# First modulation columns shared with TensorE, modulation weights in a buffer of their own on GpSimd's queue, bias rows in 16 copies

## Chip, cores and metric

One core of a Trainium2 chip runs the program. The metric is device time in microseconds, as the median of the executions shown. Lines named L… are lines of the kernel before, as its profile numbers them.

## What is computed

Two transformer blocks of two layers each run on 256 tokens of width 1024, all in float32. Of the reference, this part matters:

```python
c_act = silu(c)
for l in range(2):
    mod = c_act @ w_ada[l] + b_ada[l]                      # [1, 6144]
    sh1, sc1, gt1, sh2, sc2, gt2 = split(mod, 6)
    h = modulate(rms_norm(x, norm_mix[l]), sh1, sc1)
    p = h @ w_in[l]                                        # attention, RWKV, gated MLP, gates
    ...
    x = x + gt1 * (merged @ w_out[l])
    h = modulate(rms_norm(x, norm_ffn[l]), sh2, sc2)
    x = x + gt2 * conv_gated_ffn(h, ...)
```

The second block has no modulation. Its window attention adds `rel_bias[t5_buckets(k - q)]` to the scores, and its last step adds `(p @ w_pe_proj) * sigmoid(...)`.

## The kernel before, in words

**Products.** Activations lie with features on the partitions. A weight tile of 128x1024 comes from HBM over SP's queue into a slot `raw` (`wload`, L122 to L142). ScalarE rounds it to `hi` (L137), VectorE forms the rest `lo` (L138), and TensorE makes three products for each pair of tiles (L164 to L166), each 128x128 weights by 256 columns. The slots `raw` and `hi`/`lo` come from a ring over the open pools (`ring`): 3 `raw` and 4 splits in the mixing stages, 6 and 7 in the two feed-forward stages of the first block.

**Modulation.** A column group f (128 of the 6144 outputs) takes one 128x1024 tile of `w_ada`, which VectorE multiplies with `cact` (silu of c on all partitions) and sums along the row (L338, in the start L369). The first 16 groups of layer 0 are made at the start in `LayerA`, in 8 tiles of 1 MB on SP's queue. The other 32 of layer 0 and the 48 of layer 1 are background tasks (`ada_task`, L330 to L339): `tick` lets 0.67 of one run behind each `wload`, and `need` runs what is left up to a key before the columns are used (L389, L402). Each task takes a `raw` slot of the ring, issues its load on SP's queue (L337) and its product on VectorE right behind it.

**Start.** c comes in one row, goes through silu on ScalarE and is spread by TensorE (L1337 to L1341). The squares of x are summed on VectorE (L222), then over the partitions on TensorE (L228). `modulated` (L409 to L418) multiplies x with 1/rms (L415), applies scale and shift (L416) and splits (L201, L202). Weights 12, 6 and 10 are loaded ahead, and `fmulti` multiplies them with the contraction outermost, so that it can begin with the first of the eight tiles of h.

**Feed-forward stage of layer 0** (`ffn_a`, 372 to 617 us). `project` (L1260 to L1281) fills TensorE while the norm is under way: it splits `pT` and writes four products to DRAM over ScalarE's queue, in four buffers of the tag `pj`, three of which hold `pT`, `hi` and `lo`. Before pair 8 of 22 `hook` calls `bias_rows` (L1001 to L1015): one product gives the bias of 8 heads by distance on 8 partitions, and one DMA on ScalarE's queue writes it to DRAM with 128 copies of each row, 2 MB in all. `bias_table` (L1018 to L1024) later reads it back, shifted by one for each query, in two DMAs of 1 MB on SP's queue.

**Order of work.** Python order gives priorities, and the tile framework places each engine's instructions at build time, by its own idea of when each is ready. Each engine then runs its list in order: a VectorE instruction that waits for a DMA holds all that is behind it.

## Time and profile before

| what | value |
|---|---|
| median of 3 executions | 2324.88 us (2322.84 to 2325.23) |
| the profiled execution: span, which is the time that the profile gives for it | 2323.2 us |
| TensorE busy (matmul) | 2240.6 us, 96% |
| VectorE, ScalarE busy | 72%, 55% |
| GpSimd busy | 0.2 us |
| moved by DMA | 416.69 MB, mean 179 GB/s |

The page gives the busy time of each engine and the chain of work that ended last. A table by stretches then gives the busy time, the number of matmuls and the granted clock in a piece of the span. The order in time on one engine shows how long it stood idle before each instruction and what ended that.

### The profile page before, as it was taken

What the parts mean: (1) busy time and instruction counts of PE and PEld (TensorE: products, weight loads), DVE (VectorE), ACT (ScalarE), POOL (GpSimd) and SP (SyncE); (2) the same over time, 40 slices, a digit from 0 to 9 for tenths busy, and PEclk for the clock granted to TensorE, in tenths of its full rate; (3) what the DMA queues carried; (4) which work ended last, traced back from release to release, by engine and by line L of the source; (5) the groups of instructions that cost most, each with busy time, mean ns of one, the idle gap of its engine ahead of it and who ended that gap; (6) DMA issues with size and microseconds to landing.
All of it is one profiled execution on the core that took longest, in us unless ns stands there. A gap on an engine that the chain in (4) does not pass through costs nothing.

```text
span 2323.2 us, 46766 instructions
## 1 busy us (share of the span) xinstructions
PE 2240.6 (96%) x19122; PEld 2142.4 (92%) x19122; DVE 1677.5 (72%) x3026; ACT 1276.9 (55%) x2144; POOL 0.2 (0%) x4
## 2 busy tenths in 40 slices
PE   4999998978999999999999999999999999999999
PEld 4888898978888889999999999899999999999999
DVE  7777767757677776877576659976667655997665
ACT  4574545544457464565454457654455446666444
POOL 0000000000000000000000000000000000000000
PEclk9999999989999999999999999999999999999999
DMA  7634457777663445875576563466565556346653
GB/s 294 190 118 128 142 177 242 250 199 231 191 199 116 137 129 167 266 228 159 169 237 182 161 208 109 131 211 186 156 210 183 174 168 200 109 138 216 183 158 124
DMA packets 129117, 416.69 MB, mean 179 GB/s; under 512 B 14564, under 2 KB 20324, under 8 KB 128134
## 3 DMA queue, kind: packets, MB, share of 16 engines
q1 hardware_dynamic: 126718, 409.50, 55.8%
q10 hardware_dynamic: 2184, 4.19, 0.9%
q8 instruction: 150, 2.46, 0.4%
q14 instruction: 65, 0.53, 0.1%
HBM read 408.40 MB, written 5.24 MB: 178 GB/s over the span
## 4 chain that ended last, share of the span: by engine, by line
PE 80%; DMA 8%; DVE 7%; ACT 4%; issue 1%; SPq 0%; ACTq 0%; DVEq 0%
PE ps L164 23%; PE ps L165 22%; PE ps L166 22%; DMA raw<-in_ffn_up 3%; DVE lo L138 2%; DMA raw<-in_w_ada 2%; ACT hi L137 1%; DMA raw<-in_w_in 1%; PE rec L582 1%; PE rec L590 1%; DVE raw L369 1%; PE rec L1178 1%; DVE raw L338 1%; PE rec L636 1%; PE ps L191 1%
## 5 line engine op out<-in xcount | busy, mean ns | idle before, releaser
L164 PE MATMUL ps<-h,hi 128*128 128x256 f32 x5080 | 1438.4, 284 | 31.9 <-ACT h L201 29.6
L166 PE MATMUL ps<-h,lo 128*128 128x256 f32 x5080 | 1433.4, 283 | 14.7 <-DVE lo L138 14.7
L165 PE MATMUL ps<-l,hi 128*128 128x256 f32 x5080 | 1435.7, 283 | 4.9 <-DVE l L202 4.7
L137 ACT CAST hi<-raw 128x1024 fp32r<-128x1024 f32 (+1 forms) x724 | 704.7, 977 | 648.4 <-PE ps L165 377.8
L138 DVE TENSOR_TENSOR lo<-raw,hi 128x1024 fp32r<-128x1024 f32 (+1 forms) x724 | 818.9, 1133 | 301.6 <-ACT hi L137 299.0
L164 PEld LDWEIGHTS ps<-h,hi 128*128 128x128 f32 x5080 | 961.0, 190 | 47.2 <-ACT h L201 31.9
L166 PEld LDWEIGHTS ps<-h,lo 128*128 128x128 f32 x5080 | 962.3, 190 | 23.8 <-DVE lo L138 15.7
L165 PEld LDWEIGHTS ps<-l,hi 128*128 128x128 f32 x5080 | 961.8, 189 | 13.9 <-DVE l L202 6.8
L201 ACT CAST h<-t 128x256 fp32r<-128x256 f32 x172 | 68.6, 403 | 122.8 <-DVE t L996 96.1
L338 DVE SCALAR_TENSOR_TENSOR raw<-raw,cact 128x1024 f32<-128x1024 f32 x80 | 97.2, 1215 | 35.4 <-DMA raw<-in_w_ada 35.4
L202 DVE TENSOR_TENSOR l<-t,h 128x256 fp32r<-128x256 f32 x172 | 72.3, 423 | 60.5 <-ACT h L201 59.9
L993 DVE TENSOR_TENSOR t<-ps,r 128x512 f32<-128x512 f32 x88 | 60.8, 690 | 41.7 <-PE ps L166 41.3
L1183 DVE SCALAR_TENSOR_TENSOR cy<-cp,cwh,cy 128x256 f32<-128x256 f32 x192 | 85.0, 476 | 3.2 <-ACT cy L1181 2.9
L215 ACT ACTIVATE t<-x 128x256 f32<-128x256 f32 x96 | 38.5, 407 | 15.4 <-DVE x L964 8.5
L222 DVE TENSOR_TENSOR t<-t,t 128x256 f32<-128x256 f32 x87 | 36.4, 418 | 5.5 <-ACT t L215 4.3
L191 PE MATMUL ps<-hi,l 128*128 128x256 f32 x128 | 37.7, 294 | 0.0
L190 PE MATMUL ps<-hi,h 128*128 128x256 f32 x128 | 37.7, 294 | 0.0
L996 DVE TENSOR_TENSOR t<-t,t 128x256 f32<-128x256 f32 x88 | 36.8, 418 | 1.0 <-ACT t L995 1.0
L995 ACT ACTIVATE t<-t 128x256 f32<-128x256 f32 x88 | 36.2, 411 | 0.9
L192 PE MATMUL ps<-lo,h 128*128 128x256 f32 x128 | 36.7, 287 | 0.0
L960 ACT ACTIVATE t<-t 128x256 f32<-128x256 f32 x44 | 18.1, 415 | 29.0 <-DVE t L959 29.0
L416 ACT ACTIVATE t<-t,sh,am 128x256 f32<-128x256 f32 x32 | 18.1, 595 | 26.0 <-DVE am L395 22.5
(311 smaller groups left out, 1884.3 us busy)
## 6 DMA issues: line engine op xcount, KB each, us to landing
raw<-in_w_in SPq DMA_DIRECT2D x176, 512.0 KB, 4.2
raw<-in_ffn_in SPq DMA_DIRECT2D x176, 512.0 KB, 4.2
raw<-in_ffn_up SPq DMA_DIRECT2D x88, 512.0 KB, 5.4
raw<-in_w_ada SPq DMA_DIRECT2D x84, 512.0 KB, 4.8
raw<-in_ffn_out SPq DMA_DIRECT2D x64, 384.0 KB, 3.1
raw<-in_ffn_out SPq DMA_DIRECT2D x64, 320.0 KB, 3.2
raw<-in_w_branch SPq DMA_DIRECT2D x24, 512.0 KB, 4.1
raw<-in_ffn_down SPq DMA_DIRECT2D x32, 384.0 KB, 3.2
```

The source lines that it names most:

```text
L137: nc.scalar.copy(hi[:, :m], raw[:, :m])
L138: nc.vector.tensor_tensor(lo[:, :m], raw[:, :m], hi[:, :m], SUB)
L164: mm(ps, w[0], x[0], start=first, stop=False)
L165: mm(ps, w[0], x[1], start=False, stop=False)
L166: mm(ps, w[1], x[0], start=False, stop=last)
L191: mm(ps[:, :256], x[k][1][:, sl], h, start=False, stop=False)
L201: nc.scalar.copy(h, src)
L202: nc.vector.tensor_tensor(l, src, h, SUB)
L215: nc.scalar.square(sq, x[k])
L338: nc.vector.scalar_tensor_tensor(raw, raw, 1.0, cact, MUL, MUL, accum_out=mods[f // 8][:, f % 8:f % 8 + 1])
L993: nc.vector.tensor_tensor(v3(gu, 2), v3(ps, 2), rb, MUL)
L1183: stt(y, cp[:, jj:jj + S], cwh[:, jj * 4 + i:jj * 4 + i + 1], y, MUL, ADD)
```

## The change

Five of the 16 column groups of the start (0, 1, 2, 3 and 5) are made by TensorE, eight matmuls of one column each, from tiles that the host lays out the other way; ScalarE copies them out. The 16 tiles come one by one in the order 8, 0, 9, 1, ... with weights 12, 6 and 10 between them. c is read straight to all partitions. Half of x and `vec` come over ScalarE's queue. The sum of squares of the first norm is left to TensorE, 16 matmuls of one column. A background task loads into one buffer `adar` over GpSimd's queue, and its product is put into program order only when the next task runs, or `need` does. `bias_rows` makes 16 copies of the 8 rows in one product and writes 256 KB once; `bias_table` reads 16 pieces of 128 KB over GpSimd's queue. `project` has six buffers (`onehot` and `ohb` share them). For room, the pool `wxa` has 2 `raw` slots in place of 3, the RWKV buffers R, X, Y have 1 and ST 2, and `rkb` is made for each pair. Comments and docstrings are gone, without effect.

```diff
+ADA_BUFS = 1
+ADA_PE = (0, 1, 2, 3, 5)
     def need(self, key):
         while self.bg and self.bg[0][0] <= key:
             self.bg.pop(0)[1]()
+        self.ada_flush()
+    def ada_flush(self):
+        if self.ada_pend:
+            self.ada_pend()
+            self.ada_pend = None
+    def rms_pe(self, x):
+        nc = self.nc
+        ps = self.aux()
+        sqs = []
+        for k in range(8):
+            sq = self.tmp(S)
+            nc.scalar.square(sq, x[k])
+            sqs.append(sq)
+        self.load_ident()
+        for t in range(2):
+            for k, a in enumerate(sqs):
+                nc.tensor.matmul(ps[:, t:t + 1], a[:, t * 128:t * 128 + 128], self.ones[:, 0:1], start=k == 0, stop=k == 7)
+        return self.spread(self.inv_rms(ps[:, :2]), False)
-def ada_task(G, l, f, mods, cact):
+def ada_task(G, l, f, mods, cact, pool):
     def run():
         nc = G.nc
-        p, b = G.ring("raw")
-        raw = p.tile([128, D], F32, tag="raw", bufs=b, name=G.nm("raw"))
-        nc.sync.dma_start(raw, ...)
-        nc.vector.scalar_tensor_tensor(raw, raw, 1.0, cact, ...)
+        G.ada_flush()
+        raw = pool.tile([128, D], F32, tag="adar", bufs=ADA_BUFS, name=G.nm("ada"))
+        nc.gpsimd.dma_start(raw, ...)
+        def product():
+            nc.vector.scalar_tensor_tensor(raw, raw, 1.0, cact, ...)
+        G.ada_pend = product
 class LayerA:
-            for n, j in enumerate((0, 4, 1, 5, 2, 6, 3, 7)):
...
+            for k in range(8):
+                for f in (8 + k, k):
+                    raw = first.tile([128, D], F32, tag="ada", bufs=16, name=G.nm("raw"))
+                    out = self.mods[f // 8][:, f % 8:f % 8 + 1]
+                    if f in ADA_PE:
+                        nc.sync.dma_start(raw, G.ins["w_ada_pe"][ADA_PE.index(f)])
+                        ps = G.rec()
+                        for i in range(8):
+                            nc.tensor.matmul(ps[:, 0:1], raw[:, i * 128:i * 128 + 128], ccol[:, i:i + 1], start=i == 0, stop=i == 7)
+                        nc.scalar.copy(out, ps[:, 0:1])
+                    else:
+                        nc.sync.dma_start(raw, ...)
+                        nc.vector.scalar_tensor_tensor(raw, raw, 1.0, cact, ..., accum_out=out)
+                late(k)
-BUFS = dict(..., R=2, X=2, Y=2, W=2, ST=3, y=2)
+BUFS = dict(..., R=1, X=1, Y=1, W=2, ST=2, y=2)
 def bias_rows(G, pool):
-    sk = G.dr.tile([8, 128, 512], F32, name="skew")
-    nc.tensor.matmul(ps[0:8, :], rel, oh, start=True, stop=True)
-    nc.scalar.dma_start(sk, t.unsqueeze(1).to_broadcast([8, 128, 512]))
+    sk = G.dr.tile([128, 512], F32, name="skew")
+    nc.vector.tensor_copy(v3(rel16, 16), rel.unsqueeze(1).to_broadcast([33, 16, 8]))
+    nc.tensor.matmul(ps, rel16, oh, start=True, stop=True)
+    t = pool.tile([128, 512], F32, tag="pj", name="ohb", bufs=6)
+    nc.scalar.dma_start(sk, t)
 def bias_table(G, pool, sk):
-        G.nc.sync.dma_start(bias[:, :, q, :], src)
+        for a in range(0, 128, 16):
+            src = bass.AP(tensor=sk.tensor, offset=sk.offset + 127 - a + (128 if q == 0 else 0), ap=[[8 * 512 - 1, 16], [512, 8], [1, 256]])
+            G.nc.gpsimd.dma_start(bias[a:a + 16, :, q, :], src)
 def project(G, mp, parts, tag="pj"):
-        return mp.tile([128, 512], dt, tag=tag, name=G.nm("pj"), bufs=4)
+        return mp.tile([128, 512], dt, tag=tag, name=G.nm("pj"), bufs=6 if tag == "pj" else 4)
 def build(...):
-                nc.sync.dma_start(t, ins["x"][:, k, :])
+                (nc.scalar if k % 2 else nc.sync).dma_start(t, ins["x"][:, k, :])
...
+                    nc.sync.dma_start(cact, ins["c"].to_broadcast([128, D]))
+                    nc.scalar.dma_start(ccol, ins["cc"])
                     load_x()
+                    nc.scalar.activation(ccol, ccol, AF.Silu)
+                    nc.scalar.activation(cact, cact, AF.Silu)
+                    def late(k):
+                        if k in (1, 3, 6):
+                            load_w({1: 12, 3: 6, 6: 10}[k])
+                    G.first_rms = G.rms_pe(x)
+                    L = [LayerA(G, 0, lp, cact, sp, late, ccol)]
-                        G.weights(wx, 3, 3)
+                        G.weights(wx, 2, 3)
```

## Rows read from the trace of the kernel before

**Rows 1.** The page: span, engines, chain by engine.

```profile
span 2323.2 us, 46766 instructions
PE 2240.6 (96%) x19122; PEld 2142.4 (92%) x19122; DVE 1677.5 (72%) x3026; ACT 1276.9 (55%) x2144; POOL 0.2 (0%) x4
...
PE 80%; DMA 8%; DVE 7%; ACT 4%; issue 1%; SPq 0%; ACTq 0%; DVEq 0%
```

**Rows 2.** Stretches: from:to, us, busy PE, PEld, DVE, ACT, POOL, clock, DMA share, GB/s.

```profile
372.00:617.00 245.00, 217.98 (x1749) 214.89 (x1748) 170.99 (x289) 118.50 (x187) 0.00 (x0) 0.93 0.74 231
960.00:1178.00 218.00, 214.55 (x1793) 213.39 (x1792) 154.33 (x246) 125.80 (x204) 0.00 (x0) 0.99 0.65 205
```

**Rows 3.** The same view, pieces of the start and of the feed-forward stage.

```profile
0.00:20.00 20.00, 6.87 (x16) 3.87 (x16) 8.45 (x17) 12.05 (x18) 0.20 (x4) 1.00 0.82 291
20.00:40.00 20.00, 8.89 (x54) 8.39 (x55) 19.46 (x51) 6.00 (x12) 0.00 (x0) 1.00 1.02 413
...
500.00:520.00 20.00, 20.00 (x171) 20.00 (x170) 16.98 (x27) 11.71 (x17) 0.00 (x0) 1.00 0.92 314
...
480.00:500.00 20.00, 8.32 (x55) 8.11 (x55) 4.99 (x8) 4.21 (x6) 0.00 (x0) 0.66 0.59 148
548.00:560.00 12.00, 4.85 (x26) 3.86 (x26) 9.08 (x18) 5.57 (x11) 0.00 (x0) 0.76 0.65 191
...
560.00:580.00 20.00, 20.00 (x155) 20.00 (x154) 14.22 (x23) 8.12 (x13) 0.00 (x0) 0.89 0.81 252
```

**Rows 4.** Groups of 0 to 56 us; last product; last of the first matmuls.

```profile
L369 DVE SCALAR_TENSOR_TENSOR raw<-raw,cact 128x1024 f32<-128x1024 f32 x16 | 19.0, 1216 | 0.0
...
L228 PE MATMUL aux<-ones,t 128*128 128x1 f32 x8 | 1.9, 355 | 1.8 <-ACT cact L1341 1.8
...
45.24 1.21 DVE L369 SCALAR_TENSOR_TENSOR raw<-raw,cact 128x1024 f32<-128x1024 f32 x1
52.10 0.28 PE L165 MATMUL ps<-l,hi 128*128 128x256 f32 x1
```

**Rows 5.** Order in time behind the first products: SP's queue.

```profile
58.29 0.34 SPq L337 DMA_DIRECT2D raw<-in_w_ada  x1
60.01 1.46 SPq L133 DMA_DIRECT2D raw<-in_w_in  x2
```

**Rows 6.** Order in time around the norm of the feed-forward stage, VectorE and ScalarE.

```profile
391.75 1.23 DVE L338 SCALAR_TENSOR_TENSOR raw<-raw,cact 128x1024 f32<-128x1024 f32 x1 [1.73 <-DMA raw<-in_w_ada]
...
397.40 0.59 ACT L1280 COPY pj<-ps 128x512 f32<-128x512 f32 x1 [5.10 <-DMA proj<-pj]
```

**Rows 7.** DMA issues of 452 to 485 us: size, median us to landing.

```profile
raw<-in_ffn_up SPq DMA_DIRECT2D x6, 512.0 KB, 18.3
skew<-ohb ACTq DMA_DIRECT2D x1, 2048.0 KB
```

**Rows 8.** Order in time, waits of VectorE and TensorE at 541 to 558 us.

```profile
543.56 1.23 DVE L338 SCALAR_TENSOR_TENSOR raw<-raw,cact 128x1024 f32<-128x1024 f32 x1 [1.93 <-DMA raw<-in_w_ada]
...
553.84 0.39 PE L164 MATMUL ps<-h,hi 128*128 128x256 f32 x1 [3.72 <-ACT h L201]
```

**Rows 9.** The background products: waits, landing, and L338 in a stage (two instructions each).

```profile
  DMA raw<-in_w_ada: 35.4, 21
...
raw<-in_w_ada SPq DMA_DIRECT2D x84, 512.0 KB, 4.8
...
372.00:617.00 245.00, 34.42 (x58) 0.93 0.74 231
```

**Rows 10.** The stretch between the second mixing stage and its feed-forward stage.

```profile
940.00:980.00 40.00, 36.70 (x295) 35.94 (x293) 33.98 (x55) 20.94 (x33) 0.00 (x0) 0.96 0.82 268
```

**Rows 11.** The bias read back, and a weight that ScalarE waits for.

```profile
bias<-skew SPq DMA_DIRECT2D x2, 1024.0 KB, 7.1
...
1182.57 1.04 ACT L137 CAST hi<-raw 128x1024 fp32r<-128x1024 f32 x1 [2.21 <-DMA raw<-in_ffn_in]
```

**Rows 12.** Who waited for whom in the RWKV levels: us, times, longest.

```profile
PE rec L582 <- DVE R L575: 0.7, 2, 0.6
```

More of the change, by code (lines that the diff above doesn't have):

```diff
@@ L327, in v3, with __init__ @@
     return t.rearrange("p (a b) -> p a b", a=a)
[L332 removed]
+def ada_task(G, l, f, mods, cact, pool):
     def run():
         nc = G.nc
[L335 to L338 removed]
+        G.ada_flush()
+        raw = pool.tile([128, D], F32, tag="adar", bufs=ADA_BUFS, name=G.nm("ada"))
+        nc.gpsimd.dma_start(raw, G.ins["w_ada"][l, f // 2, :, (f % 2) * D:(f % 2) * D + D])
+        def product():
+            nc.vector.scalar_tensor_tensor(raw, raw, 1.0, cact, MUL, MUL, accum_out=mods[f // 8][:, f % 8:f % 8 + 1])
+        G.ada_pend = product
     return run
 class LayerA:
[L345 removed]
+    def __init__(self, G, l, pool, cact, first=None, late=None, ccol=None):
         nc = G.nc
@@ L349, in __init__ @@
         self.vec = p.tile([128, NVA], F32, tag="vec", name=G.nm("vec"))
-        nc.sync.dma_start(self.vec, G.ins["va"][l])
+        (nc.sync if first is None else nc.scalar).dma_start(self.vec, G.ins["va"][l])
         self.mods = [p.tile([128, 8], F32, tag=f"mod{i}", name=G.nm("mod")) for i in range(6)]
@@ L356, in __init__ @@
         else:
-            for n, j in enumerate((0, 4, 1, 5, 2, 6, 3, 7)):
-                if n == 6:
-                    late()
-                raw = first.tile([128, 2, D], F32, tag="ada", bufs=8, name=G.nm("raw"))
-                src = v3(G.ins["w_ada"][l, j], 2)
-                if n < 6:
-                    nc.sync.dma_start(raw, src)
-                for h in range(2):
-                    if n >= 6:
-                        nc.sync.dma_start(raw[:, h, :], src[:, h, :])
-                    f = 2 * j + h
-                    nc.vector.scalar_tensor_tensor(raw[:, h, :], raw[:, h, :], 1.0, cact, MUL, MUL, accum_out=self.mods[f // 8][:, f % 8:f % 8 + 1])
-        G.bg += [((l, f), ada_task(G, l, f, self.mods, cact)) for f in range(0 if first is None else 16, 48)]
+            for k in range(8):
[9 more added lines that the diff above has]
+                    else:
+                        nc.sync.dma_start(raw, G.ins["w_ada"][l, f // 2, :, (f % 2) * D:(f % 2) * D + D])
+                        nc.vector.scalar_tensor_tensor(raw, raw, 1.0, cact, MUL, MUL, accum_out=out)
+                late(k)
+        G.bg += [((l, f), ada_task(G, l, f, self.mods, cact, p)) for f in range(0 if first is None else 16, 48)]
     def load_small(self):
@@ L410, in modulated @@
     nc = G.nc
-    r = G.rms(x, False, True)
+    r = G.first_rms
+    if r is None:
+        r = G.rms(x, False, True)
+    G.first_rms = None
     out = []
@@ L515, in rwkv_pair @@
     ps = G.rec()
-    mm(ps[:, :S], L.rkblk[p], rk, start=True, stop=True)
+    rkb = mp.tile([128, 128], F32, tag="rkb", name=G.nm("rkb"), bufs=1)
+    ts(rkb, G.c("blk", 128), 64.0, L.col("r_k", p), MUL, MUL)
+    mm(ps[:, :S], rkb, rk, start=True, stop=True)
     yield 0.6
@@ L747, in mix_a @@
     nc.vector.tensor_scalar(L.lnb, L.cols("ln_b", 4), float(D), None, MUL)
-    L.rkblk = []
-    for p in range(4):
-        t = mp.tile([128, 128], F32, tag=f"rkb{p}", name=G.nm("rkb"))
-        nc.vector.tensor_scalar(t, G.c("blk", 128), 64.0, L.col("r_k", p), MUL, MUL)
-        L.rkblk.append(t)
     def pair(i):
@@ L1003, in bias_rows @@
     nc = G.nc
-    oh = pool.tile([33, 512], F32, tag="oh", name="onehot")
+    oh = pool.tile([128, 512], F32, tag="pj", name="onehot", bufs=6)[:33, :]
     nc.sync.dma_start(oh, G.ins["onehot"])
@@ L1334, in build @@
                     G.weights(sp, 3, 2)
-                    crow = sp.tile([1, D], F32, name="crow")
-                    nc.sync.dma_start(crow, ins["c"])
-                    nc.scalar.activation(crow, crow, AF.Silu)
-                    for i in range(2):
-                        ps = G.aux()
-                        nc.tensor.matmul(ps, G.ones[0:1, :], crow[:, i * 512:i * 512 + 512], start=True, stop=True)
-                        nc.scalar.activation(cact[:, i * 512:i * 512 + 512], ps, AF.Copy, scale=float(D))
-                    load_x()
-                    load_w(12)
-                    load_w(6)
-                    L = [LayerA(G, 0, lp, cact, sp, lambda: load_w(10))]
+                    ccol = sp.tile([128, 8], F32, name="ccol")
+                    nc.sync.dma_start(cact, ins["c"].to_broadcast([128, D]))
+                    nc.scalar.dma_start(ccol, ins["cc"])
+                    load_x()
+                    nc.scalar.activation(ccol, ccol, AF.Silu)
[5 more added lines that the diff above has]
+                    L = [LayerA(G, 0, lp, cact, sp, late, ccol)]
                     G.wps.pop()
@@ L1507, in arrays @@
     out["c"] = i["c"]
+    out["w_ada_pe"] = np.stack([i["w_ada"][0][:, f * 128:f * 128 + 128].reshape(8, 128, 128).transpose(1, 0, 2).reshape(128, D) for f in ADA_PE])
+    out["cc"] = np.ascontiguousarray(_feat(i["c"][0]))
     out["w_ada"] = np.ascontiguousarray(i["w_ada"].reshape(L, D, 24, 2, 128).transpose(0, 2, 4, 3, 1)).reshape(L, 24, 128, 2048)
```

14 lines of the change are left out of this document (6 added, 8 removed).

## The prediction

> **What bounds the kernel now.** I read the page first. TensorE is busy 2240.6 of 2323.2 us, and 80% of the chain that ended last runs over it [rows 1]. So time can come only from where TensorE stands idle or runs slowly, some 83 us of idle time in all.
>
> The table by stretches shows where. The two feed-forward stages of the first block do nearly the same work, 1749 and 1793 matmuls, but the first takes 245.0 us and the second 218.0 [rows 2]. At the second's pace the first would take 1749 / 1793 x 218.0 = 212.7 us, so 32 us are lost in it. The second has no `bias_rows`, and the background tasks run out early in it. Full pace is 171 matmuls in 20 us [rows 3], 0.117 us each.
>
> The other loss is the start. VectorE is full between 20 and 40 us, 19.46 of 20, while TensorE is busy 8.89 us [rows 3]. The 16 modulation products take VectorE 1.216 us each, the last ends at 45.24 + 1.21 = 46.45 us, and TensorE's first weights are done at about 52.2 us [rows 4].
>
> **The change, part by part.**
>
> *Start.* VectorE loses 5 of 16 products, 5 x 1.2 = 6.1 us, and the sums of squares. Then the DMAs bind. They moved 20 x 291 = 5.8 MB in the first 20 us and 413 GB/s after that [rows 3]. What must land before the last product is x 1.05 MB, three weights 3.15, sixteen tiles 8.39, c spread over the partitions 0.52 and small things 0.17, together 13.3 MB. The remaining 7.5 MB take 18.1 us, so the last tile lands at about 38.1 us. Its product ends 1.3 us later, and from there to the end of the first weights I take what it is now, 52.2 - 46.45 = 5.8 us. That gives 45.2 us, a gain of 7. The 11 products left on VectorE (13.4 us) fit between the landings. On TensorE come 40 matmuls of one column; the nearest row is L228, 8 in 1.9 us [rows 4], so 9.5 us, beside loads. They cost only where one waits for its tile with ready products behind it in the queue. At worst they add all 9.5 us: 2.5 us lost. At best only 3 us follow the last landing: 11 gained. ScalarE issues six DMAs more and eight short copies and activations; it is idle more than half of this time, which hides them.
>
> *Behind the start.* A background load is issued at 58.29 us, and the next weight only gets its slot at 60.01 [rows 5]. With that load out of the ring the weight goes 1.7 us earlier. I take 2 with what follows; between 0 and 3.
>
> *Norm of the first feed-forward stage.* Two waits lie in it: VectorE waits 1.73 us for a background tile and then spends 1.2 on it, with the reciprocal behind, and ScalarE waits until 397.40 us, 5.10 us, for a buffer of `project`, with the scaled tiles of h behind it [rows 6]. Six buffers leave three free for outputs in place of one. Part of the waits overlaps the norm itself, which stays: I take 4, between 0 and 5.
>
> *Bias rows.* While 2 MB go out, the median weight needs 18.3 us to land, where a tile of this size usually takes 4.8 [rows 7, 9], and between 480 and 500 us TensorE makes 55 matmuls in place of 171, at a granted clock of 0.66 on average, so partly at 1.2 GHz and not 2.4 [rows 3]: (171 - 55) x 0.117 = 13.6 us. An eighth of the bytes is written, from 128 partitions. The copy to 16 column groups and a product as long as before cost under 1 us, beside weights that are there. I take 14, with little around it; between 10 and 15.
>
> *Background products.* VectorE waits 35.4 us for their tiles, 21 times [rows 9], with splits and h behind them. At 541 to 558 us that reaches TensorE: VectorE waits 1.93 us, and TensorE 3.72 for an h made late behind it [rows 8]. From 548 to 560 it makes 26 matmuls of a possible 103, and in the next 20 us 155 of 171 [rows 3]: (77 + 16) x 0.117 = 10.9 us. Now the product stands 1.5 weights behind its load, so the tile should be there. SP is relieved of 80 issues, and GpSimd, busy 0.2 us in all [rows 1], has nothing else. New is a loop: the next load waits for the product that empties the only buffer. Its period is 4.8 us to land [rows 9] + 1.2. The stage has 29 products in 245 us [rows 9], one in 8.4 us, so it fits. In the down products a weight is 33 matmuls, and one product comes every 1.5 x 33 x 0.117 = 5.8 us; there the loop falls back by 0.2 us on each of some 11, 2 us. `need` forces what is pending, with the scale columns behind it on VectorE, but by then the load is a weight old. The tile must not wait long for GpSimd, and no row has a load on its queue. I bound it by the nearest, 4.8 us, and by twice that. Taken: 9.5 gained, which leaves 1.4 for the loop; between 5 and 11.
>
> The Trainium skill ("DMA: Bandwidth & Descriptors", section "Anatomy of one DMA — SWDGE (gpsimd) path") gives about 2.0 us plus bytes at 436 GB/s for such a load, by which I estimate 3.2 us for a tile. By it the loop would never fall back, and the gain would be 1.4 us larger; no row here can show it.
>
> *The two boundaries* at 617 and 960 us have background products between the last x and the norm. From 940 to 980 us 295 matmuls run of a possible 342 [rows 10], 5.5 us lost, most of it the norm. For both I take 3; between 0 and 5.
>
> *Bias read back.* It lands 7.1 us after its issue on SP's queue, and a weight behind it is waited for by 2.21 us [rows 11]. Sixteen pieces on GpSimd's queue move the same bytes beside the weights, needed only in the attention much later. I take 1; from 1 lost to 3 gained.
>
> *Fewer RWKV buffers.* TensorE waits only 0.7 us in all for R [rows 12], and R is rebuilt when its product is done. I take 0; up to 4 lost. One `raw` slot less in the feed-forward stages is what the background tiles gave up.
>
> *Sum:* 7 + 2 + 4 + 14 + 9.5 + 3 + 1 = 40.5 us. The three terms of the first feed-forward stage, 27.5, stay below the 32 of its twin. The profiled execution goes from 2323.2 to 2282.7 us; the median stands 1.7 above it, so 2284.
>
> **Rivals.**
>
> *The start gains nothing*, because TensorE's new products hold the queue or the loads come later: 2284 + 7 = 2291. For it: DMA already runs at 413 GB/s there. Against: VectorE is the full one [rows 3].
>
> *The hole at 550 us stays*, because the one-buffer loop stalls VectorE in the down products: 2284 + 9.5 = 2293.5. For it: 6.0 against 5.8 us.
>
> *The bias write is not the cause* of the slow weights, or its new form is as slow, so that this part doesn't do what it says: 2284 + 14 = 2298. Against: the landing times [rows 7].
>
> *All the terms at their best:* 11 + 3 + 5 + 15 + 11 + 5 + 3 = 53, so 2272.
>
> *Slower: GpSimd's loads take twice as long*, since VectorE, busy 72% [rows 1], keeps GpSimd from issuing them. Landing in 9.6 us makes a loop of 10.8, and 29 x (10.8 - 8.4) = 70 us on VectorE's queue in the first feed-forward stage: 2284 + 70 = 2354. It decides from 29 x (loop - 8.4) = 40.5 on, a loop of 9.8 us, so 8.6 to land. Against: GpSimd is idle, and transfers now land in 4.8. The Trainium skill ("SBUF — State Buffer", section "Who interferes with whom") says that a DMA from this queue is starved of descriptors while VectorE runs an instruction in a two-port mode. By it only copies and tensor-scalar instructions would count, no term of the loop in this stage; no run here shows it.
>
> **How the numbers follow.** A measurement can tell about 0.2%, 5 us. Forecast 0.50; no gain at the start 0.15; the hole stays 0.13; the bias write 0.06; all at their best 0.06; no change, by losses spread over all parts, 0.04; GpSimd slow 0.06. Faster is 0.50 + 0.15 + 0.13 + 0.06 + 0.06 = 0.90. The first two rivals together give 2300.5, the third with a miss of 6 elsewhere 2304; the best case less a little gives 2268. So the range is 2268 to 2304.
>
> **What would show it.** Right: the last VectorE product of the start before 41 us and the first weights done by 46; no ScalarE wait for `proj<-pj`; `skew` landing in a few us and 171 matmuls from 480 to 500 us; no VectorE wait for background tiles in the first feed-forward stage, which takes some 218 us. Wrong: waits on `adar` of several us, each with `lo` behind it; TensorE idle behind one-column matmuls; the second layer's mixing stage longer than now by waits for R or X.

## The result and the profile after

The changed kernel takes 2341.5 us (2339.0 to 2342.3) against 2325.1 in the same comparison: 1.0068 of the time before, with an interval of 1.0055 to 1.0080. It is 16 us slower; the forecast was 41 us faster.

The page first: span and engines, then the chain by engine, as in [rows 1].

```profile
span 2339.4 us, 47085 instructions
PE 2259.6 (97%) x19222; PEld 2164.3 (93%) x19222; DVE 1668.7 (71%) x3011; ACT 1274.3 (54%) x2147; POOL 51.1 (2%) x100
...
PE 74%; issue 17%; DMA 3%; DVE 2%; ACT 2%; POOL 1%; SPq 0%; ACTq 0%; POOLq 0%; DVEq 0%
```

TensorE is busy 19 us longer and has 100 matmul records more. The page doesn't tell where the time went. Four moments do, taken from the order in time. The first z ends the start; it is ScalarE's first reading of the first weights' products. The other three are VectorE's first scaling `t<-x,aux` in a norm.

| moment | before | after | later by |
|---|---|---|---|
| first z | 51.8 us | 74.2 us | 22.4 |
| norm of the first feed-forward stage | 394.4 | 420.4 | 26.0 |
| norm of the second layer's mixing stage | 620.6 | 644.0 | 23.4 |
| norm of the second feed-forward stage | 979.3 | 998.7 | 19.4 |
| end of the span | 2323.2 | 2339.4 | 16.2 |

So the start loses 22 us, where 7 were to be gained. The first feed-forward stage, from its norm to the next, gains 2.6 us (226.2 to 223.6), where some 30 were to be gained. In the table by stretches the first two lines answer to the start in [rows 3], the next two to 480 to 520 us there, the last to the hole.

```profile
0.00:20.00 20.00, 6.80 (x31) 6.64 (x31) 4.41 (x15) 6.61 (x12) 1.77 (x7) 1.00 0.89 306
20.00:40.00 20.00, 16.32 (x77) 16.20 (x76) 10.72 (x24) 4.32 (x10) 0.73 (x2) 1.00 1.03 410
...
480.00:500.00 20.00, 20.00 (x171) 20.00 (x170) 16.55 (x28) 7.32 (x13) 2.11 (x4) 1.00 0.69 226
500.00:520.00 20.00, 20.00 (x171) 20.00 (x170) 15.85 (x28) 10.19 (x16) 1.58 (x3) 1.00 0.80 250
560.00:580.00 20.00, 10.96 (x69) 10.20 (x70) 14.64 (x29) 8.25 (x14) 1.58 (x3) 0.74 0.73 238
```

The write of the bias rows no longer holds anything: 171 matmuls from 480 to 500 us, where before there were 55. VectorE is no longer full in the start, as forecast, yet the start is later. And there is a hole at 560 to 580 us with 69 matmuls. What is new in the start is in the groups of 0 to 76 us, which answer to [rows 4]:

```profile
L395 PE MATMUL rec<-ccol,raw 128*128 128x1 f32 x80 | 17.2, 345 | 0.0
L399 DVE SCALAR_TENSOR_TENSOR raw<-raw,cact 128x1024 f32<-128x1024 f32 x11 | 13.2, 1217 | 3.2 <-DMA raw<-in_w_ada 3.2
L366 DVE SCALAR_TENSOR_TENSOR ada<-ada,cact 128x1024 f32<-128x1024 f32 x8 | 9.8, 1222 | 11.7 <-DMA ada<-in_w_ada 11.7
...
L396 ACT COPY mod<-rec 128x1 f32<-128x1 f32 x5 | 0.8, 159 | 24.5 <-PE rec L395 24.5
```

Two things stand there. TensorE's five columns are 80 records, not 40, and busy it for 17.2 us; ScalarE waits 24.5 us for the five results, in its queue ahead of the casts of the first weights. And L366, the *background* product, is in the start eight times, with 11.7 us of waiting. Before, the first one came at 62.29 us. The view of the background tile shows the whole run of it: first and last start of the loads and products, and what each engine waited for.

```profile
L363 POOL DMA_DIRECT2D ada<-in_w_ada x80: 527/527/698, 1.3 to 629.6; - x80
L366 DVE SCALAR_TENSOR_TENSOR ada<-ada,cact x80: 1183/1225/1228, 8.0 to 634.4; 128x1024 f32<-128x1024 f32 x80
...
  DMA ada<-in_w_ada: 76.7, 48
...
DMA to landing us min/median/max: 3.7/4.5/8.5
```

The loads begin at 1.3 us and are done by 630; before, the products ran to 999 us. That is one in 7.9 us. VectorE waits 76.7 us for their tiles, 48 times; in [rows 9] it was 35.4 us in 21. The tiles land as fast as before (4.5 us against 4.8). What has gone is the pacing. Before, each load needed a slot of the weight ring, behind weights on SP's queue. Now it needs only its own buffer on a queue that has nothing else, so the builder places it, and the product, as soon as the buffer is free by its own idea of the times. VectorE then stands before 48 of the 80 tiles, in order. In the hole at 560 us it looks like this (order in time, VectorE, then TensorE):

```profile
554.93 1.23 DVE L366 SCALAR_TENSOR_TENSOR ada<-ada,cact 128x1024 f32<-128x1024 f32 x1 [0.56 <-DMA ada<-in_w_ada]
560.71 1.23 DVE L366 SCALAR_TENSOR_TENSOR ada<-ada,cact 128x1024 f32<-128x1024 f32 x1 [0.53 <-DMA ada<-in_w_ada]
566.64 1.23 DVE L366 SCALAR_TENSOR_TENSOR ada<-ada,cact 128x1024 f32<-128x1024 f32 x1 [0.68 <-DMA ada<-in_w_ada]
```

```profile
563.89 0.58 PE L174 MATMUL ps<-h,hi 128*128 128x256 f32 x1 [4.56 <-ACT h L211]
569.86 0.58 PE L174 MATMUL ps<-h,hi 128*128 128x256 f32 x1 [4.70 <-ACT h L211]
```

One product every 5.9 us, each with a wait: the loop of one buffer runs at its own period, not at that of the weights. But these waits are short, 0.5 to 0.7 us where [rows 8] has 1.93, and TensorE's waits are longer than there, 4.56 and 4.70 us for 3.72. So the hole itself isn't shown to come from the background products. The two other small parts, the skew write and the bias read, look like this:

```profile
bias<-skew POOLq DMA_DIRECT2D x16, 128.0 KB, 11.4
...
skew<-ohb ACTq DMA_DIRECT2D x1, 256.0 KB, 3.5
```

The write lands in 3.5 us. The read takes longer than in [rows 11] (11.4 us a piece for 7.1); GpSimd alone waits for it, 7.5 us in 5.

### The profile page after: what moved, and what is told of

The parts are those of the page before. It is cut to its first block, busy times and chain, and to the rows that moved or that the text cites. A ratio compares the mean times of both kernels' runs of the same rounds, so it can differ in the third digit from the quotient of the medians.

```text
span 2339.4 us, 47085 instructions
## 1 busy us (share of the span) xinstructions
PE 2259.6 (97%) x19222; PEld 2164.3 (93%) x19222; DVE 1668.7 (71%) x3011; ACT 1274.3 (54%) x2147; POOL 51.1 (2%) x100
## 3 DMA queue, kind: packets, MB, share of 16 engines
HBM read 408.92 MB, written 3.41 MB: 176 GB/s over the span
## 4 chain that ended last, share of the span: by engine, by line
PE 74%; issue 17%; DMA 3%; DVE 2%; ACT 2%; POOL 1%; SPq 0%; ACTq 0%; POOLq 0%; DVEq 0%
PE ps L174 21%; PE ps L175 21%; PE ps L176 20%; POOL ada L363 1%; PE rec L1212 1%; DMA ada<-in_w_ada 1%; PE rec L626 1%; PE rec L618 1%; ACT hi L141 1%; DMA x<-in_x 1%; PE ps L201 1%; DVE lo L142 1%; PE rec L395 1%; PE ps L200 1%; PE ps L202 1%
## 5 line engine op out<-in xcount | busy, mean ns | idle before, releaser
L366 DVE SCALAR_TENSOR_TENSOR ada<-ada,cact 128x1024 f32<-128x1024 f32 x80 | 97.7, 1221 | 76.8 <-DMA ada<-in_w_ada 76.7
L1024 DVE TENSOR_TENSOR t<-ps,r 128x512 f32<-128x512 f32 x88 | 60.7, 690 | 37.8 <-PE ps L176 37.5
L363 POOL DMA_DIRECT2D ada<-in_w_ada x80 | 42.4, 530 | 587.3 <-DVE ada L366 512.9
```

The costliest lines, as they stand in the source:

```text
L363: nc.gpsimd.dma_start(raw, G.ins["w_ada"][l, f // 2, :, (f % 2) * D:(f % 2) * D + D])
L366: nc.vector.scalar_tensor_tensor(raw, raw, 1.0, cact, MUL, MUL, accum_out=mods[f // 8][:, f % 8:f % 8 + 1])
```

## The experiments

Three explanations were open at first. **A**: the background loads run ahead and cost VectorE its time in order. **B**: TensorE's columns cost the start. **C**: the smaller buffers cost. The table gives all kernels; the stage is the first feed-forward stage, from its norm to the next. First z, norm and stage are from one profiled execution each, the ratio to the kernel before is of all executions.

| kernel | first z | norm | stage | median | ratio (interval) |
|---|---|---|---|---|---|
| before | 51.8 | 394.4 | 226.2 | 2325.1 | |
| after | 74.2 | 420.4 | 223.6 | 2341.5 | 1.0068 (1.0055 to 1.0080) |
| e1_old_start | 60.5 | 407.7 | 224.3 | 2331.1 | 1.0023 (1.0006 to 1.0041) |
| e2_old_ada | 64.0 | 408.7 | 214.5 | 2323.8 | 0.9998 (0.9986 to 1.0010) |
| e3_rest_only | 51.1 | 394.9 | 214.5 | 2313.6 | 0.9942 (0.9923 to 0.9961) |
| e4_paced | 64.1 | 426.2 | 230.3 | 2395.4 | 1.0301 (1.0278 to 1.0324) |
| e5_no_pe | 53.1 | 397.3 | 212.0 | 2309.5 | 0.9938 (0.9923 to 0.9953) |
| e6_gate_first | 51.7 | 405.3 | 224.0 | 2332.1 | 1.0030 (1.0015 to 1.0044) |
| e7_two_bufs | 51.1 | 406.2 | 227.4 | 2337.8 | 1.0058 (1.0043 to 1.0073) |
| e8_own_sp | 51.3 | 393.0 | 225.6 | 2319.8 | 0.9982 (0.9967 to 0.9997) |
| e9_ring_pool | 50.9 | 397.6 | 223.4 | 2328.1 | 1.0020 (1.0008 to 1.0032) |
| e10_dve_copy | 64.5 | 407.8 | 215.0 | 2327.4 | 1.0010 (0.9998 to 1.0022) |
| e11_no_pe_big | 53.9 | 398.1 | 209.7 | 2308.4 | 0.9928 (0.9914 to 0.9942) |
| e12_bias_only | 52.6 | 394.9 | 210.3 | 2309.2 | 0.9930 (0.9914 to 0.9946) |
| e13_two_on_pe | 60.7 | 405.5 | 208.8 | 2320.4 | 0.9984 (0.9969 to 0.9999) |
| e14_pool_delay | 60.8 | 414.7 | 239.0 | 2351.1 | 1.0110 (1.0089 to 1.0131) |
| e15_old_start_big | 51.6 | 395.6 | 213.9 | 2312.6 | 0.9944 (0.9925 to 0.9964) |
| e16_after_no_pe | 61.9 | 408.7 | 221.5 | 2332.0 | 1.0039 (1.0023 to 1.0055) |
| e17_last_on_pe | 65.2 | 409.9 | 216.6 | 2330.8 | 1.0025 (1.0008 to 1.0042) |

### Taking the change apart: start and background task

**e1_old_start**

```diff
-            for k in range(8):
-                for f in (8 + k, k):
...
+            for n, j in enumerate((0, 4, 1, 5, 2, 6, 3, 7)):
```

> Edit: the changed kernel with the start of before (all 16 first products on VectorE, x and c loaded as before, norm as before); the background loads stay in their own buffer on GpSimd's queue. Theory A (the background loads are no longer held back: they begin in the first microsecond and come about every 8 us instead of every 11.75, taking DMA time and VectorE's in-order time from the start and the first mixing stage): the loads still come early, most of the loss stays, about 2325 to 2335 us, first norm of the first FFN stage at 410 or later. Theory B (TensorE's one-column products hold ScalarE and TensorE in the start): the loss is gone, about 2300 us, norm of the first FFN stage at about 395. Theory C (the smaller buffers): about 2340, as the changed kernel.

**e2_old_ada**

```diff
-        raw = pool.tile([128, D], F32, tag="adar", bufs=ADA_BUFS, name=G.nm("ada"))
-        nc.gpsimd.dma_start(raw, G.ins["w_ada"][l, f // 2, :, (f % 2) * D:(f % 2) * D + D])
+        p, b = G.ring("raw")
+        raw = p.tile([128, D], F32, tag="raw", bufs=b, name=G.nm("raw"))
+        nc.sync.dma_start(raw, G.ins["w_ada"][l, f // 2, :, (f % 2) * D:(f % 2) * D + D])
```

> Edit: the changed kernel with the background task of before (load on SyncE's queue into the shared weight slots, product at once); the new start stays. Theory A: about 2290 to 2300 us, no background tile before 60 us, the start no later than before (last first product by about 45 us). Theory B: ScalarE still waits over 20 us for the one-column results and the start ends about 10 to 18 us later than before; with the faster bias rows and projection the sum is about 2315 to 2325. Theory C: about 2325 to 2340.

**e3_rest_only** has both edits.

> Edit: the changed kernel with both the start and the background task of before; bias rows in 16 copies, bias read on GpSimd's queue, six projection buffers and the smaller buffers stay. Theories A and B: the parts that stay give what was forecast for bias rows and projection, 14 to 20 us less than before, about 2305 to 2311 us; the second half of the first FFN stage shows no stretch of 20 us with under 140 matmuls but the one at 541 to 560. Theory C: no gain, 2325 us or more.

Against e3, the new start costs 13 us by the ratios (0.9998 to 0.9942), the new background task 19 (1.0023 to 0.9942). Both together, 32, less the 13.5 that the rest gains, would be 18.5; the changed kernel is 16 slower. So the losses nearly add up: A and B are both there, and neither alone. The first z says the same: 51.1 with neither, 60.5, 64.0, and 74.2 with both. C falls: the rest gains 0.6%, though less than forecast.

### TensorE's columns

**e5_no_pe**: e2 with `ADA_PE = ()`.

```diff
-ADA_PE = (0, 1, 2, 3, 5)
+ADA_PE = ()
```

> Edit: the kernel with the new start and the old background task, but none of the first columns is made by TensorE: VectorE makes all 16, in the new order, with the rest of the new start (x over two queues behind the broadcast of c, squares summed by TensorE, weights spread between the columns). Measured so far: the new start costs 14 us by the first FFN norm (408.7 against 394.9 us with the old start). Theory B (TensorE's one-column products: ScalarE waits 23.5 us for five results and the split of the first weights stands behind those waits): the loss is gone, first FFN norm at 392 to 397 us, total 2306 to 2314. Theory D (the late and reordered loads of x, c and the weights): the loss stays, norm at 405 to 409, total 2320 to 2326.

The first z falls from 64.0 to 53.1 us and the time to 0.9938, as with the old start. So, as far as the times can tell, all that the new start costs is TensorE's columns; the new order of x, c and weights makes the first z 2 us later and costs nothing in the total. Which property of the columns? ScalarE's waits were the nearest suspect, so VectorE made the copies:

**e10_dve_copy**

```diff
-                        nc.scalar.copy(out, ps[:, 0:1])
+                        nc.vector.tensor_copy(out, ps[:, 0:1])
```

> Edit: the kernel with the new start and the old background task (2324 us), with the five one-column results of TensorE copied by VectorE instead of ScalarE. Theory B1 (the cost of TensorE's products is ScalarE standing 23.5 us in front of its copies, with the splits of the first weights behind it): splits of the first weight begin by 21 us instead of 26.6, first FFN norm at 396 to 401 us, total 2309 to 2316. Theory B2 (the cost is TensorE itself, 3.4 us for each column at the lower clock, between the first products, and the wait for the column's load in its queue): norm at 405 to 409, total 2320 to 2327.

The wait moved over to VectorE (16.6 us in 5) and the first z stayed at 64.5. So the casts behind ScalarE's copies are not it.

**e13_two_on_pe** has `ADA_PE = (0, 1)`.

> Edit: the kernel with the new start and the old background task, with two of the first columns on TensorE instead of five. Theory B2 (each column takes TensorE 3.4 us at the lower clock, in order between the first products, and the start waits for it): the loss goes with the number, two fifths of it: first mixing results (the first z) at about 57 to 59 us (64.0 with five, 53.1 with none), total 2313 to 2318. Rival B3 (any column on TensorE makes the ring of waits TensorE, ScalarE, VectorE, TensorE, and the number matters little): first z at 61 to 65 us, total 2319 to 2325.

**e17_last_on_pe** has `ADA_PE = (5, 14, 6, 15, 7)`.

> Edit: the kernel with the new start and the old background task, with TensorE making five of the last columns (5, 6, 7, 14, 15) in place of five of the first (0, 1, 2, 3, 5). Theory B2 (the time on TensorE): the same five groups stand among the first products, first z at 61 to 65 us, total 2319 to 2326. Theory B3 (the ring of waits: a late column result holds ScalarE and VectorE, and with them the tiles that TensorE's queue waits for): the first six tiles of h no longer hang on TensorE, first z at 54 to 59 us, total 2309 to 2317.

In e13 the first z (60.7 us) lies between the two theories and the total (2320.4) in B3's range; in e17 the total (2330.8) lies above both, and the first z (65.2) just above B2's range. The groups of TensorE's columns and the first z, for five first, two first and five last columns:

```profile
L391 PE MATMUL rec<-ccol,raw 128*128 128x1 f32 x80 | 15.6, 325 | 0.0
...
64.02 0.47 ACT L461 ACTIVATE z<-ps,omm 128x256 f32<-128x256 f32 x1
```

```profile
L391 PE MATMUL rec<-ccol,raw 128*128 128x1 f32 x32 | 7.0, 348 | 0.0
...
60.68 0.47 ACT L461 ACTIVATE z<-ps,omm 128x256 f32<-128x256 f32 x1
```

```profile
L391 PE MATMUL rec<-ccol,raw 128*128 128x1 f32 x80 | 10.8, 265 | 0.0
...
65.21 0.47 ACT L461 ACTIVATE z<-ps,omm 128x256 f32<-128x256 f32 x1 [5.63 <-PE aux L176]
```

Against 53.1 us with none, two columns cost 7.5 us for 7.0 us of TensorE, five first 10.9 for 15.6, five last 12.1 for 10.8. The time on TensorE is of the right size but not in proportion. The order in time shows more of the steps. First VectorE in e2, two of its waits and its last product of the start:

```profile
25.27 0.16 DVE L420 TENSOR_TENSOR sh<-mod,vec 128x2 f32<-128x2 f32 x1 [2.58 <-ACT mod L392]
38.90 0.16 DVE L420 TENSOR_TENSOR sh<-mod,vec 128x2 f32<-128x2 f32 x1 [5.54 <-ACT mod L392]
...
56.59 1.22 DVE L395 SCALAR_TENSOR_TENSOR raw<-raw,cact 128x1024 f32<-128x1024 f32 x1
```

In e5 VectorE makes five products more, and its last one starts at 45.74 us, 10.9 us earlier; the first z is 10.9 us earlier too. VectorE's list holds `sh`, the shift columns of two tiles of h, ahead of its own products, and `sh` waits for ScalarE's copy of TensorE's column: 2.58 + 5.54 + 1.75 = 9.9 us in three waits in e2, none in e5. TensorE in turn reaches the third and the later columns only behind products of the first tiles of h, which wait for the columns before. So in e2 the loss is on VectorE, by the ring that B3 names. In e17 the first tiles don't hang on TensorE, and B3's times failed; but the last two do. There VectorE has done its products by 38.2 us, TensorE reaches the last column at 55.62 us, behind products of the tiles before, and `sh` waits for it until 57.70. So a column costs what stands behind it in three in-order lists, and not only TensorE's time for it. That any columns on TensorE cost this start 7 to 12 us is shown; the share of each step in e13 and e17 is open.

**e16_after_no_pe**: the changed kernel with `ADA_PE = ()`.

> Edit: the changed kernel in full, but VectorE makes all 16 first columns. If the costs of TensorE's columns (14 us) and of the background loads (own buffer, GpSimd's queue, early start; 18 us) add up: 2325 to 2331, first z at about 61 to 64 us. If they overlap, that is, if the early loads alone would fill the start: 2333 to 2342, first z over 68 us.

2332.0 us, first z 61.9: between the two ranges in the total, 7 us below the changed kernel by the ratios (1.0039 to 1.0068), and in the first z as for adding up. Here the columns cost half of the 14 us that they cost without the early loads. In the start they overlap with nothing (the first z is 12.3 us earlier without them, 74.2 to 61.9), so the other half is made up later; where is not shown. The early loads alone hold the start by 9 us (61.9 against 53.1 in e5).

### The background loads: when, buffer or queue

**e4_paced**

```diff
+        nc.gpsimd.tensor_copy(raw[:, 0:1], G.gate[:, 0:1])
         nc.gpsimd.dma_start(raw, G.ins["w_ada"][l, f // 2, :, (f % 2) * D:(f % 2) * D + D])
```

> Edit: the changed kernel, but one column of the background buffer is first written by GpSimd from the newest weight tile's high part, so that a load can't start before that weight has been split: the loads keep their place in the program. 80 copies of 128x1 are added on GpSimd. Theory A: the loads follow the weights again (one per about 11.75 us, the last near 1000 us), VectorE's waits for the tiles fall from 76.7 us in 48 to under 40 us, and the time falls by 20 to 40 us to 2300 to 2320. Theory B: the pacing changes only the first FFN stage by a few us, 2330 to 2340. Theory C: 2335 to 2345.

A miss, and the most useful one. The loads were paced (the copies run from 71.2 to 1068.3 us), and the kernel lost 54 us more. Its costliest groups:

```profile
L368 DVE SCALAR_TENSOR_TENSOR ada<-ada,cact 128x1024 f32<-128x1024 f32 x80 | 97.6, 1220 | 134.9 <-DMA ada<-in_w_ada 134.7
...
L364 POOL COPY ada<-hi 128x1 f32<-128x1 f32 x80 | 47.1, 589 | 954.6 <-ACT hi L141 669.5 <-DVE ada L368 172.5 <-DVE Q L631 49.1
```

VectorE's waits for the tiles grew to 134.7 us. So a late load is worse here than an early one, which points at VectorE standing before the tile and not at the early transfers.

**e6_gate_first** holds only the first load in this way, with the old start.

> Edit: old start, new background task, but the first background load alone is held until the first weight behind the start has been split (one 128x1 copy on GpSimd); the later loads run free. Theory A1 (early loads share the DMA engines and VectorE with the start): the first FFN norm falls from 407.7 to 395 to 400 us, the first FFN stage stays at about 224 us (214.5 with the old task), total 2319 to 2326. Theory A2 (the denser loads cost VectorE wherever they run, the start is nothing special): norm at 404 to 408 us, total 2328 to 2333.

The start came back (first z 51.7), but nothing else did: VectorE stood 6.27 us before the held tile at 69 us and 76.1 in all. By the norm (405.3 us) and the total A2 came in, but not by its reason that the start is nothing special: the early loads do cost the start 9 us, and 12 us are lost soon after, in the first mixing stage.

**e7_two_bufs** adds a second buffer in the feed-forward stages (for room, `rel16` lies in a work buffer).

```diff
+        ps = [pool] + G.adax
+        G.nada += 1
+        raw = ps[G.nada % len(ps)].tile([128, D], F32, tag="adar", bufs=ADA_BUFS, name=G.nm("ada"))
```

> Edit: as the kernel that holds the first background load, and in the FFN stages a second background buffer, used in turn with the first. Theory A3 (one buffer makes VectorE stand before each tile for most of a load): VectorE's waits for background tiles in the first FFN stage fall from 53 us in 32 to under 15 us, and that stage from about 224 to 214 to 217 us, total 7 to 10 us below the kernel with one buffer. Theory A2 (the rate of the loads, not the buffer): the loads come denser still, the stage stays at 222 us or more.

VectorE's waits in the stage are still 45.1 us in 27 (51.8 in 33 in e6), and the stage is longer, 227.4 us: A3 falls, and A2 comes in. One buffer instead of two is not the cause.

**e8_own_sp** (own buffer, old queue) and **e9_ring_pool** (ring slots, new queue) complete the square, all with the old start.

```diff
-        nc.gpsimd.dma_start(raw, G.ins["w_ada"]
+        nc.sync.dma_start(raw, G.ins["w_ada"]
```

> Edit: old start, new background task with its own buffer and its late product, but the loads go over SyncE's queue between the weights, as before. Theory A (the idle queue lets the loads run ahead): the loads are paced by the queue again, about one in 11.75 us, none before 55 us; first FFN norm at 393 to 397 us, VectorE's waits for the tiles under 35 us, total 2305 to 2314. Rival (the own single buffer is the cost, whatever the queue): waits of 70 us or more, first FFN norm over 404 us, total 2325 to 2333.

> Edit: old start and the background task of before (shared weight slots, product at once), but its loads go over GpSimd's queue. Together with the kernels measured so far (own buffer on GpSimd's queue 2331 us, own buffer on SyncE's queue 2320 us, shared slots on SyncE's queue 2314 us) this is the fourth corner. Theory A2 (the loads cost where they run ahead of the weights; shared slots hold them back on any queue): 25 to 27 tiles in the first FFN stage, that stage at 213 to 217 us, total 2310 to 2318. Rival (GpSimd's queue itself costs 11 us, as between the two kernels with an own buffer): total 2322 to 2330, the first FFN norm at 404 us or later.

| | SyncE's queue | GpSimd's queue |
|---|---|---|
| ring slots, product at once | 0.9942 (e3) | 1.0020 (e9) |
| own buffer, product later | 0.9982 (e8) | 1.0023 (e1) |

Theory A in its first form fell in both, and so did the rival in e8 (63.3 us of waits, 2319.8 us) and the norm of the rival in e9 (397.6 us). In e8 the loads run ahead on SP's queue too (39.3 to 655.1 us), and the cost is 9 us. So the buffer of their own is enough to unpace them; the idle queue isn't needed. In e9 they are held back by the ring (57.9 to 996.4 us), and GpSimd's queue costs 18 us all the same; with an own buffer it costs 9.5 (e1 against e8). The tiles land in 4.5 and 4.7 us at the median. One difference is ahead of the issue: with an own buffer, from the end of a product to the issue of the next load. First e8, then the changed kernel (VectorE's last instruction of the product, then the issue):

```profile
331.10 0.08 DVE L366 DVE_READ_ACCUMULATOR ada<-ada,cact 128x1 f32 x1
...
331.21 0.33 SPq L363 DMA_DIRECT2D ada<-in_w_ada  x1
```

```profile
60.88 0.08 DVE L366 DVE_READ_ACCUMULATOR ada<-ada,cact 128x1 f32 x1
...
61.26 0.53 POOL L363 DMA_DIRECT2D ada<-in_w_ada  x1 [5.09 <-DVE ada L366]
```

That is 331.21 - 331.18 = 0.03 us on SP and 61.26 - 60.96 = 0.30 us on GpSimd; over all loads the medians are 0.03 and 0.30. From the issue to the product that waits for it, both take 4.6 us. VectorE waits for some 45 tiles, so 45 x 0.27 = 12 us. To test that, the lag was doubled:

**e14_pool_delay**

```diff
+        nc.gpsimd.memset(raw[:, 0:1], 0.0)
         nc.gpsimd.dma_start(raw, G.ins["w_ada"][l, f // 2, :, (f % 2) * D:(f % 2) * D + D])
```

> Edit: the kernel with the old start and the own buffer on GpSimd's queue (2331 us), with one more GpSimd instruction (a memset of one column of the buffer) between the release of the buffer and the issue of each load, so that every load is issued some 0.2 to 0.4 us later. Theory Q (GpSimd's queue costs because it issues the load 0.30 us after the product's end instead of 0.04, and VectorE, which waits for 45 of 80 tiles, stands that much longer each time; 45 x 0.26 = 11.7 us, as measured between the two queues): VectorE's waits for the tiles grow from 74 by 9 to 18 us, total 2338 to 2350. Rival (the queue costs by its descriptors or by its share of the DMA engines, not by the moment of the issue): waits and total stay within 4 us of 74 and 2331.

The view of the background tile in e14 (loads; VectorE's waits; landing):

```profile
L364 POOL DMA_DIRECT2D ada<-in_w_ada x80: 527/527/698, 1.3 to 659.4; - x80
...
  DMA ada<-in_w_ada: 90.4, 46
...
DMA to landing us min/median/max: 3.7/4.4/8.9
```

The lag went from 0.30 to 0.57 us, the landing stayed, VectorE's waits grew from 74.1 to 90.4 us, and the kernel by 20 us, just above the forecast, with whatever the builder moved besides. So a later issue costs. That the lag is what GpSimd's queue costs isn't shown by this, and by stages it doesn't come out (the start ends with the first z, the first mixing stage with the norm; the waits are VectorE's for background tiles, in us and times):

| kernel | start | first mixing stage | its waits | feed-forward stage | its products | its waits |
|---|---|---|---|---|---|---|
| e3_rest_only | 51.1 us | 343.8 us | 5.9 in 8 | 214.5 us | 25 | 34.0 in 17 |
| e8_own_sp | 51.3 | 341.7 | 5.8 in 7 | 225.6 | 36 | 53.8 in 31 |
| e9_ring_pool | 50.9 | 346.7 | 12.7 in 11 | 223.4 | 25 | 43.2 in 20 |
| e6_gate_first | 51.7 | 353.6 | 21.8 in 13 | 224.0 | 34 | 51.8 in 33 |
| e1_old_start | 60.5 | 347.2 | 15.3 in 12 | 224.3 | 34 | 53.0 in 32 |
| e14_pool_delay | 60.8 | 353.9 | 16.6 in 11 | 239.0 | 34 | 66.8 in 32 |

In the feed-forward stage, where most of the waits lie, e1 and e8 wait equally long and take equally long, whatever the queue. e1 loses its time to e8 before: 9 us in the start, where its loads begin at 1.3 us and those of e8 at 39.3, and 5.5 in the first mixing stage. e6, with the start of e8, loses 12 us in that stage. Why GpSimd's queue costs there stays open. In e14 the stage grows by 14.7 us for 32 waits, more than 32 x 0.27 = 8.6. With an own buffer 34 or 36 products fall into the stage instead of 25, and it takes 10 to 11 us more than in e3; but e9, with 25, takes 9 more.

The kernels with the new bias rows and without TensorE's columns show how tightly VectorE is held, by its waits for background tiles over the whole execution:

| kernel | waits | median |
|---|---|---|
| e12_bias_only | 38.4 us | 2309.2 us |
| e11_no_pe_big | 40.8 | 2308.4 |
| e5_no_pe | 41.3 | 2309.5 |
| e15_old_start_big | 44.6 | 2312.6 |
| e3_rest_only | 46.2 | 2313.6 |
| e8_own_sp | 63.3 | 2319.8 |
| e9_ring_pool | 67.5 | 2328.1 |
| e7_two_bufs | 68.4 | 2337.8 |
| e1_old_start | 74.1 | 2331.1 |
| e16_after_no_pe | 75.6 | 2332.0 |
| e6_gate_first | 76.1 | 2332.1 |
| e14_pool_delay | 90.4 | 2351.1 |

From the first to the last, 52.0 us of waits go with 41.9 us of time, 0.8 us each. All the others lie within 10 us of that line (e8 9.5 us below it). So over queue, buffer, gate and delay the loss goes with these waits. That they are its whole cause is not shown.

### The rest, and the version that beats both

**e12_bias_only**: the kernel before with `bias_rows` and `bias_table` of the change alone; `onehot` and `ohb` share the four buffers of `project`.

> Edit: the kernel before with the bias rows in 16 copies and the bias read in 16 loads on GpSimd's queue alone; four projection buffers, start, background task and all other buffers as before. Forecast in the prediction: 14 us for the write (the second half of the first FFN stage) and 1 for the read: 2308 to 2312, first FFN stage at 210 to 214 us instead of 226. Rival (the six projection buffers bring the greater part of the 11.7 us that the stage gained with both): 2316 to 2322, stage over 218 us.

**e11_no_pe_big** and **e15_old_start_big** have the buffer counts of before.

```diff
-Q=4, R=1, X=1, Y=1, W=2, ST=2, y=2)
+Q=4, R=2, X=2, Y=2, W=2, ST=3, y=2)
...
-                        G.weights(wx, 2, 3)
+                        G.weights(wx, 3, 3)
```

> Edit: the candidate for a version that beats both: the new start with all 16 columns on VectorE, the old background task, bias rows in 16 copies, six projection buffers, and the buffer counts of before (two of R, X and Y, three of ST, three further weight slots in the FFN stages). Theory C (the smaller buffers cost something): 4 to 8 us below the same kernel with the smaller buffers (2309.5), 2300 to 2306. Rival (one buffer each is enough): 2307 to 2312.

> Edit: the kernel with the old start and the old background task, bias rows in 16 copies and six projection buffers, with the buffer counts of before (it had the smaller ones at 2313.6). Theory C (the third weight slot of the FFN stages is worth the 4 us between the stages of 214.5 and 210.3 us): stage at 208 to 212 us, total 2305 to 2311. Rival: 2311 to 2315.

e12 takes 0.9930 of the time before, 16 us less, with the stage at 210.3 us: the bias rows and their reading alone bring all of the gain. Theory C fell in e11 and e15, and both rivals came in. Six projection buffers (e15), the new start without TensorE (e5, e11) and the smaller buffers (e3, e5) have intervals that overlap with that of e12 and with each other's. So e12 is the version to keep: 16 us faster than before and 32 faster than the changed kernel, by one part of the change. In its stage the hole at 540 to 560 us stays:

```profile
480.00:500.00 20.00, 20.00 (x170) 20.00 (x170) 14.16 (x23) 9.62 (x16) 0.00 (x0) 1.00 0.69 222
540.00:560.00 20.00, 16.58 (x119) 15.82 (x120) 14.30 (x24) 10.05 (x17) 0.00 (x0) 0.79 0.78 241
```

## Why the prediction was wrong, step by step

- **Start (forecast 7 us gained, at worst 2.5 lost): wrong.** In the changed kernel the first z is 22.4 us later. The failed step is "On TensorE come 40 matmuls of one column; the nearest row is L228, 8 in 1.9 us [rows 4], so 9.5 us, beside loads". The eight records of L228 were four matmuls of the program, since each such fp32 matmul leaves two records. Five columns are 80 records and 17.2 us, so the worst case was nearly 8 us too small. "They cost only where one waits for its tile with ready products behind it in the queue" failed too: they cost 14 us (e2 against e5) with no wait of TensorE for a column's tile in e2's profile. What waits is VectorE, 9.9 us for their results, with its own products behind.
- **The sum of bytes in the start** counted 13.3 MB, and none of the background tiles. Seven of them, 3.7 MB, were issued by 61.3 us, four, 2.1 MB, before 46 us: at 410 GB/s some 5 us of transfers among those of the start. e1 shows the early loads alone: its last product of the start begins 4.7 us later than in e3 (49.3 against 44.5), its first z 9.4 later (60.5 against 51.1). From 39 to 58 us VectorE makes three background products there, with 4.0 us of waits for two of them, and from 40 to 60 us TensorE makes 93 matmuls at a granted clock of 0.74 where e3 has 130 at 1.00; what each of these costs is not separated. No row could show the loads, but the reading of the diff could.
- **Background products (forecast 9.5 us gained): wrong, and the main step.** "Now the product stands 1.5 weights behind its load, so the tile should be there" took Python's order for the order on the engines. With an own buffer nothing ties a load to a weight, on SP's queue either (e8). "So it fits" took the need (one in 8.4 us) for the rate: the loop made 33 products in the 223.6 us of the stage, one in 6.8 us, and VectorE waited for 31 of them. Cost 19 us (e1 against e3): 9 for the buffer (e8 against e3), 9.5 for the queue (e1 against e8). The forecast gain rested on the hole at 550 us, and that stayed though VectorE's waits in it fell to 0.5 to 0.7 us.
- **The slower rival** named GpSimd's queue and the right place, VectorE's queue, with the wrong price: loads that take 9.6 us to land. They land in 4.5. The loss came far below the point that I gave, from an unpaced loop in VectorE's order; how GpSimd's queue adds to it is open. The Trainium skill ("DMA: Bandwidth & Descriptors", section "Anatomy of one DMA — SWDGE (gpsimd) path") gave an estimate of 3.2 us for a tile; the trace has 3.7 at least and 4.5 at the median, beside the loads of weights, so here the measurement decides.
- **Bias rows (14) and read (1): right together.** 15.7 us by e12, 15.9 of it in the stage of the write (226.2 to 210.3 us); the write lands in 3.5 us, and 171 matmuls run from 480 to 500 us. The read was not timed by itself.
- **Norm of the first feed-forward stage (4): the mechanism came, the gain did not.** No ScalarE wait for `proj<-pj` is left with six buffers; with four (e12) it is 3.5 us, and the time is the same.
- **The hole at 550 us** stayed in every kernel, in e12 too, and moved to 560 to 580 us here. **RWKV buffers (0): right**; TensorE waits 0.6 us for R. The ring slot (2) and the two boundaries (3) were not tried by themselves.

## What to carry to other kernels

A load that gets its own buffer loses what paced it, even on the old queue (e8): ask what holds it back then, and where an in-order engine will stand and wait for it. If work is moved to an engine that looks idle in the average, count its records in that stretch, and what stands behind them in its queue. When a change has several parts, time the part with the clearest row by itself: here it was worth more than the whole.

## What was not expected of the hardware

- A load on GpSimd's queue is issued 0.30 us after the buffer's release, on SP's 0.03 us; its instruction takes 0.53 us against 0.33. From issue to landing the two are equal (4.4 and 4.5 us, e1 and e8). The Trainium skill ("DMA: Bandwidth & Descriptors", section "Latency and other measured facts") puts the first byte of the GpSimd path at about 1 us and of the other at 0.6; the 0.4 us between them doesn't show in these landing times, though a lag of like size shows ahead of the issue.
- One column of 16 records took TensorE 3.41 to 3.55 us in four of five cases in e2 and 1.84 in the fifth. The matmuls beside them tell why (TensorE in order, a slow and a fast column):

```profile
31.00 3.41 PE L391 MATMUL rec<-ccol,raw 128*128 128x1 f32 x16
34.63 0.41 PE L176 MATMUL ps<-h,lo 128*128 128x256 f32 x1
34.84 0.41 PE L175 MATMUL aux<-l,hi 128*128 128x256 f32 x1
...
47.31 0.28 PE L174 MATMUL aux<-h,hi 128*128 128x256 f32 x1
47.43 0.28 PE L175 MATMUL aux<-l,hi 128*128 128x256 f32 x1
47.67 1.84 PE L391 MATMUL rec<-ccol,raw 128*128 128x1 f32 x16
```

Beside the slow column a 128x256 matmul starts every 0.21 us, beside the fast one every 0.12: all of TensorE's work runs at about half the pace. The table by stretches has the granted clock at 1.00 from 20 to 40 us all the same. In e17 a column of 3.41 us, among matmuls 0.21 us apart, lies in a stretch with a granted clock of 0.50, the lower of the two levels (41.4 to 44.9 us). So the pace in e2 is that of the lower level, as two expectations say, and the column of the granted clock doesn't show it there; why not stays open.
